# A hybrid diffusion block on one core: when the last squares are summed, where the first down piece lies, and how the last product ends

## The chip, the cores and the metric

The kernel runs on one core of one Trainium2 chip. The metric is the device time of one execution in microseconds (us), taken as the median of several runs. The engines are TensorE (PE in the profile; its weight loads are PEld), VectorE (DVE), ScalarE (ACT), GpSimd (POOL) and SyncE (SP), which here only issues DMAs. A matmul writes to PSUM, which has eight banks of 512 fp32 columns per partition; everything else lies in SBUF or in device memory.

## The reference

One layer of a diffusion backbone on 512 latent tokens and 256 context tokens, of width 1024:

```
h_lat = modulate(x, norm1_g, sh1, sc1)          # RMSNorm * (1 + scale) + shift
h_ctx = modulate(ctx, norm1_g, csh1, csc1)
o_lat = token_mixer(h_lat, h_ctx, ...)          # one input projection, then:
    ssd = rmsnorm(y_ssd * silu(z), ssd_norm_g)  #   bidirectional SSD, 4 groups, 2048 channels
    att = windowed attention + context + sink
    out = (sig_ssd * (ssd @ w_o_ssd) + sig_att * (att @ w_o_att)) @ w_out
x = x + gt1 * o_lat
x = x + gt2 * conv_ffn(modulate(x, norm2_g, sh2, sc2))   # up 1024 -> 2 x 2816, conv, silu gate, down
return rmsnorm(x, final_g)
```

The six modulation vectors come from `silu(c) @ w_mod + b_mod`.

## The kernel before

**Precision.** A product of two fp32 matrices is three matmuls: both operands are split in a high and a low part, and high x high, high x low and low x high are added (L193, L194 and L196 in `gemm`; L1861 to L1863 in `down`). A weight piece of 128 x 1024 is loaded on SP's queue into one of three raw buffers ("wraw"), then `split` makes the high part on ScalarE (L149) and the low part on VectorE (L150). High and low go to the buffers "whi" and "wlo", two of each, unless `ELSEWHERE` names another place for that piece. `run` walks a list of steps, each with the names of its weight pieces, and loads one piece ahead.

**Order.** Each engine works through its own instructions in order. PE's order is written out by hand in some stages (`tc.manual_schedule`), among them the whole of `down`. Elsewhere the order on an engine is chosen when the kernel is built, from program order and an estimate of when each instruction can start; `tc.keep_in_program_order` pins an instruction behind those pinned before it on its engine.

**SSD branch and its norm.** The gated rows yz of the SSD branch come in four groups of four row blocks. Their squares are summed into one tile, `ssq`: `square` lets ScalarE square a block (L1333) and GpSimd add it to `ssq` (L1336). For the last group (`late` false) these four squares stand next to the output projection.

**Output projection of the SSD branch.** `y_split` loads the sixteen blocks of yz, scales them and splits them to `yh` (ScalarE, L1525) and `yl` (VectorE, L1526). `os_first` computes the first two output row blocks in two passes over the channels; its PE order is written out. Piece ("os", 2) has its high and low part in a part of `yh[3]` that isn't filled yet, which is why its subtraction shows as `yh<-wraw,yh`. At the end of the first pass `rms_sums_of([ssq])` sums `ssq` over the partitions on PE (L238); root and spreading (L248, L249, L255) follow, giving `F["rs"]`. `os_step(o)` for o = 2 to 7 does the other row blocks: `merge_rows` loads three gate rows (ts_d, ta_d, ao_d) on SP, `gates` (L1540, L1541) combines them with `F["rs"]`, a gemm of 48 matmuls follows, then `merge`. Between these steps `weave` puts the steps on the modulation weights (`msteps[8:18]`): each loads a piece of w_mod (the raw buffer shows as `wraw<-wm`) and multiplies and adds it on VectorE (L554, L556).

**Feed-forward.** `up_step` runs 22 times, with the convolution on ScalarE and VectorE after its products (L1756 to L1758 read PSUM). `down` computes the down projection as seven products of half-size matrices (`ORDER` = p1, p3, p6, p7, p5, p2, p4), each of six weight pieces g = 0 to 5 and two token tiles t = 0, 1 (g = 5 has half the width): 42 `ITEMS`. `prepared(i)` loads and splits piece i up to `AHEAD` = 4 pieces ahead; the first piece, ("dn", 0), is split by `run` as any other, into "whi" and "wlo". `operand` gives the tokens' side, for some products loaded from device memory into a ring. `block` issues the matmuls of one piece on one tile, `product` those of one product. Each accumulator is one PSUM bank from `accb()`.

**The end.** The last product, p4, gives two tiles of 128 tokens x 512 columns. For each tile, behind all of PE's work: two VectorE operations (L1981, L1982), a square with its sum on ScalarE (L1904), `root` (L1916, L1917 on VectorE, L1918 on GpSimd), the scaling (L1985 on VectorE, L1987 on ScalarE for the columns that were finished before) and the output DMAs (L1922 in `put`).

Of the kernel before, what the change touches and what calls it, by code (L numbers as in the profile page):

```python
# [18 lines left out]
P = 128  # L19
# [25 lines left out]
def tile_hybrid_layer(  # L45
# [1276 lines left out]
    def square(late=True):  # L1322

        yz = SQUARES.pop(0)
        if "ssq" not in F:
            F["ssq"] = [ssq]
            tc.keep_in_program_order(S.activation(ssq, yz, AF.Square))
        else:

            tag = "th" if late or len(F["ssq"]) % 4 == 0 else "E"  # L1330
            sq = bp.tile([P, 512], F32, tag=tag, name="sq", bufs=3 if tag == "E" else 1)
            F["ssq"].append(sq)
            a = S.activation(sq, yz, AF.Square)  # L1333
            if late:
                tc.keep_in_program_order(a)
            G.tensor_tensor(ssq, ssq, sq, ALU.add)  # L1336
# [220 lines left out]
    def os_first(x):  # L1557

        def fn(*w):
            if x == 0:  # L1560
                F["os"] = accb(), accb()
            else:
                rows = [merge_rows(o) for o in range(2)]


            first = [(0, o, range(4)) for o in range(2)] if x else [(0, i % 2, (i // 2,)) for i in range(8)]
            with tc.manual_schedule(engines={mybir.EngineType.PE}):
                for u, o, ks in first + [(1, o, range(4, 8)) for o in range(2)]:
# [200 lines left out]

    ELSEWHERE["up", 1] = far_piece  # L1770

# [48 lines left out]
    def prepared(i):  # L1820
# [27 lines left out]
    def down(w0):  # L1848
# [5 lines left out]

        def block(i, bank, t, first, last):
            hi, lo, x = READY[i]
            n, g = ITEMS[i]
            for j in range(pairs(g)):
                h, l = x(j)
                z, r = slice(512 * j, 512 * j + 512), tok(t)  # L1860
                T.matmul(bank[t], h[:, r], hi[:, z], start=first and g == 0 and j == 0, stop=False, skip_group_check=True)  # L1861
                T.matmul(bank[t], l[:, r], hi[:, z], start=False, stop=False, skip_group_check=True)  # L1862
                T.matmul(bank[t], h[:, r], lo[:, z], start=False, stop=last and g == 5, skip_group_check=True)  # L1863

        def product(n, bank, first, last, between={}):
            i0 = 6 * ORDER.index(n)
            seq = [(g, t) for g in range(6) for t in range(2)]
            if n == "p4":
                seq = seq[:8] + [(g, t) for t in range(2) for g in range(4, 6)]
            for g, t in seq:  # L1870
                if t == 0:
                    for k in range(i0 + g, i0 + g + AHEAD):
                        if 1 < k < len(ITEMS) and k not in READY:
                            if ITEMS[k] == ("p2", 0):
                                space()
                            prepared(k)
                block(i0 + g, bank, t, first, last)
                if t == 1 and g in between:
                    between[g]()

# [8 lines left out]
        def space():  # L1889
            F["ring"] = F["c2"].tile([P, 2, NP2, HL], F32R, tag="xl", name="ring").rearrange("p a b c -> p (a b c)")  # L1890
            F["ring"] = F["ring"][:, : 4 * 1024].rearrange("p (r a b c) -> p r a b c", r=4, a=2, b=2)
            F["fg"] = F["c2"].tile([P, 2, NP2, HL], F32, tag="xh", name="fgb").rearrange("p a b c -> p (a b c)")[:, :D]
# [10 lines left out]
        def square_sum(t, c, y):  # L1903
            S.activation(tmp("tm"), y, AF.Square, accum_out=ss3[:, t, c : c + 1])  # L1904
            XO[t, c] = y
# [6 lines left out]

        def root(t):
            rs = cpool.tile([P, 4], F32, tag="rs", name="rs", bufs=2)[:, :1]
            ms = cpool.tile([P, 4], F32, tag="ms", name="ms", bufs=2)[:, :1]
            V.tensor_tensor(ms, ss3[:, t, 0:1], ss3[:, t, 1:2], ALU.add)  # L1916
            V.tensor_scalar(ms, ms, 1.0 / D, EPS, ALU.mult, ALU.add)  # L1917
            G.tensor_tensor(rs, ms, phalf[:, 0:1], ALU.pow)  # L1918
# [5 lines left out]
        def finish(t):  # L1924
            rs = root(t)
            for c in range(2):
# [3 lines left out]
        with tc.manual_schedule(engines={mybir.EngineType.PE}):  # L1930
            m = [accb(), accb()]
            product("p1", m, True, True)
            sa = snap(m, "tb")
            f_ = [accb(), accb()]
            product("p3", f_, True, True)
# [7 lines left out]
            for t in range(2):  # L1943
# [5 lines left out]
                {  # L1949
                    0: lambda: update(0, 1, f[0]),  # L1950
                    1: lambda: update(1, 1, f[1]),
                    2: lambda: update(2, 1, hs[0]),
                    3: lambda: update(3, 1, hs[1]),
                },
# [4 lines left out]
            def early(t):  # L1959
# [5 lines left out]
                V.tensor_tensor(y, y, F["fg"][:, CH[1]], ALU.mult)  # L1965

            def third():
# [7 lines left out]
            product(  # L1975
                "p4", h, False, True,
                {0: lambda: update(0, 0, sa[0]), 1: lambda: update(1, 0, sa[1]), 2: third, 3: fourth},
            )
            for t in range(2):
                y = XO[2 + t, 0] = tmp("ta")  # L1980
                V.tensor_tensor(y, h[t], F["g2"][0], ALU.mult)  # L1981
                V.tensor_tensor(y, y, sb[t], ALU.add)  # L1982
                square_sum(2 + t, 0, y)
                rs = root(2 + t)
                V.scalar_tensor_tensor(y, y, rs, F["fg"][:, CH[0]], ALU.mult, ALU.mult)  # L1985
                put(2 + t, 0)
                S.activation(XO[2 + t, 1], XO[2 + t, 1], AF.Copy, scale=rs)  # L1987
                put(2 + t, 1)

# [6 lines left out]
    def tok(t):  # L1996
# [101 lines left out]
```

## Time and profile before

| what | us |
|---|---|
| median of 3 runs | 1255.89 |
| the runs | 1256.02, 1255.89, 1253.77 |
| the profiled execution | 1256.97 |
| its span in the profile | 1255.2 |
| PE busy in the span | 1229.2 |
| VectorE busy | 920.6 |
| ScalarE busy | 683.2 |
| GpSimd busy | 174.7 |
| mean granted clock of TensorE | 0.995 |

Times in the profile count from the start of the span, so 749.09 means 749.09 us after it. A row of the timeline gives the start, the duration, the engine, the line of the kernel and the operation with its output and inputs, then how many of them follow each other (x3) and, in brackets, how long the engine sat idle before it and what ended that. A row of a group gives the number of instructions with their shortest, median and longest duration in ns. A row of windows gives the busy time of PE, PEld, DVE, ACT and POOL with the number of instructions, then the granted clock, the share of the DMA engines that was busy, and GB/s. A matmul's own duration is longer than the distance to the next, since matmuls are pipelined.

### The profile page before, as it was taken

Reading aid. Unit: us, or ns where it says so; the run is one execution under the profiler, and the core shown is the slowest. Engines: PE = TensorE matmul, PEld = TensorE weight load, DVE = VectorE, ACT = ScalarE, POOL = GpSimd, SP = SyncE. Lnnn points to the kernel's source line nnn. Section 1 sums busy time; section 2 is a strip of 40 time slices with the busy share of each in tenths; the row PEclk is TensorE's granted clock in tenths of the full one; section 3 lists DMA queues with packets and bytes.
Section 4 is the critical chain, followed back from the end, with each engine's and each line's share of the span. In section 5 each row is a group of like instructions: output and inputs, shape, how many; then the busy total and the mean of one; then the engine's idle time right before and its main releaser. Section 6 shows DMA issues by size and latency. Waiting matters only on the chain.

```text
span 1255.2 us, 17458 instructions
## 1 busy us (share of the span) xinstructions
PE 1229.2 (98%) x6292; PEld 1010.6 (81%) x6292; DVE 920.6 (73%) x1517; ACT 683.2 (54%) x1286; POOL 174.7 (14%) x177
## 2 busy tenths in 40 slices
PE   7999999999999999999999999999999999999997
PEld 4698888888888878778777777888988888887885
DVE  4856887888654697787787777777678888886566
ACT  3557887887445366475475654223545444445443
POOL 0000111121100034252452540000200000000000
PEclk9999999999999999999999999999999999999999
DMA  9652568877845234354355567777145444457685
GB/s 340 231 172 86 183 212 186 222 189 211 223 141 186 93 102 127 119 163 155 113 139 171 155 213 253 240 253 246 47 143 184 163 141 151 151 167 250 220 287 199
DMA packets 109494, 226.74 MB, mean 181 GB/s; under 512 B 9568, under 2 KB 48800, under 8 KB 109408
## 3 DMA queue, kind: packets, MB, share of 16 engines
q1 hardware_dynamic: 101920, 199.42, 48.8%
q0 software_dynamic: 6912, 25.17, 8.5%
q8 instruction: 49, 0.80, 0.3%
q10 hardware_dynamic: 576, 1.05, 0.2%
q14 instruction: 37, 0.30, 0.1%
HBM read 194.34 MB, written 50.92 MB: 195 GB/s over the span
## 4 chain that ended last, share of the span: by engine, by line
PE 84%; DVE 7%; POOL 3%; ACT 2%; DMA 2%; issue 2%; SPq 0%; POOLq 0%; DVEq 0%; ACTq 0%
PE acc L196 17%; PE acc L193 17%; PE acc L194 17%; PE acc L1861 3%; PE acc L1862 3%; PE acc L1863 3%; PE score L784 3%; PE po L833 3%; PE pt L820 2%; PE mis L408 2%; PE mis L1452 1%; PE mis L1446 1%; DVE wlo L150 1%; PE acc L903 1%; PE acc L904 1%
## 5 line engine op out<-in xcount | busy, mean ns | idle before, releaser
L150 DVE TENSOR_TENSOR wlo<-wraw,whi 128x1024 fp32r<-128x1024 f32 (+2 forms) x123 | 154.9, 1260 | 72.4 <-ACT whi L149 68.3
L193 PE MATMUL acc<-hlh,whi 128*128 128x512 f32 x488 | 200.1, 410 | 0.0
L196 PE MATMUL acc<-hlh,wlo 128*128 128x512 f32 x488 | 191.3, 392 | 0.0
L194 PE MATMUL acc<-hll,whi 128*128 128x512 f32 x488 | 190.8, 391 | 0.0
L149 ACT CAST whi<-wraw 128x1024 fp32r<-128x1024 f32 (+2 forms) x123 | 126.6, 1031 | 115.2 <-PE acc L194 62.1
L193 PE MATMUL acc<-mh,whi 128*128 128x512 f32 x368 | 143.7, 390 | 0.0
L196 PE MATMUL acc<-mh,wlo 128*128 128x512 f32 x368 | 143.2, 389 | 0.0
L194 PE MATMUL acc<-ml,whi 128*128 128x512 f32 x368 | 143.2, 389 | 0.0
L196 PEld LDWEIGHTS acc<-hlh,wlo 128*128 128x128 f32 x488 | 91.6, 188 | 20.2
L194 PEld LDWEIGHTS acc<-hll,whi 128*128 128x128 f32 x488 | 91.9, 188 | 18.2 <-issue 2.4
L193 PEld LDWEIGHTS acc<-hlh,whi 128*128 128x128 f32 x488 | 91.8, 188 | 17.7 <-issue 2.4
L194 PEld LDWEIGHTS acc<-ml,whi 128*128 128x128 f32 x368 | 69.1, 188 | 14.6 <-issue 0.2
L193 PEld LDWEIGHTS acc<-mh,whi 128*128 128x128 f32 x368 | 69.1, 188 | 14.5 <-issue 0.2
L196 PEld LDWEIGHTS acc<-mh,wlo 128*128 128x128 f32 x368 | 69.1, 188 | 14.3
L793 DVE CUSTOM_DVE_ANT_0 p<-score,winm,nsink 128x512 f32<-128x512 f32 (+1 forms) x64 | 51.9, 810 | 15.3 <-PE score L784 13.8
L1239 DVE SCALAR_TENSOR_TENSOR ta<-acc,half,ta 128x511 f32<-128x511 f32 (+1 forms) x66 | 43.8, 664 | 21.6 <-ACT ta L1238 21.5
L800 ACT ACTIVATE p<-p,mneg 128x512 f32<-128x512 f32 (+1 forms) x64 | 49.7, 777 | 15.4 <-DVE mneg L793 14.9
L1238 ACT ACTIVATE ta<-acc,half 128x512 f32<-128x512 f32 (+1 forms) x66 | 46.5, 705 | 20.8 <-PE acc L196 19.5
L193 PE MATMUL acc<-hch,whi 128*128 128x256 f32 x176 | 54.4, 309 | 0.0
L1357 POOL TENSOR_TENSOR st<-st,eT 128x512 f32<-128x512 f32 x24 | 29.2, 1218 | 177.3 <-ACT st L1374 159.2
L828 DVE TENSOR_TENSOR ptl<-pt,pth 128x512 fp32r<-128x512 f32 x72 | 47.5, 686 | 8.5 <-ACT pth L824 7.7
L556 DVE SCALAR_TENSOR_TENSOR tm<-wraw,csil,tm 128x512 f32<-128x512 f32 x56 | 41.9, 748 | 15.5 <-DMA wraw<-wm 14.9
(453 smaller groups left out, 2950.4 us busy)
## 6 DMA issues: line engine op xcount, KB each, us to landing
wraw<-wup SPq DMA_DIRECT2D x44, 512.0 KB, 3.9
wt_d<-wdn POOLq DMA_DIRECT2D x36, 512.0 KB, 7.8
fb<-cs_d SPq DMA_DIRECT2D x32, 512.0 KB, 5.9
wraw<-wm SPq DMA_DIRECT2D x32, 512.0 KB, 3.8
wraw<-wx SPq DMA_DIRECT2D x24, 512.0 KB, 3.5
wraw<-wt_d SPq DMA_DIRECT2D x20, 512.0 KB, 4.4
sp_d<-te SPq DMA_DIRECT2D x33, 256.0 KB, 2.1
wm<-wm SPq DMA_DIRECT2D x16, 512.0 KB, 8.0
```

Source lines behind the costliest of these rows:

```text
L149: S.copy(hi[:, :n], r[:, :n])
L150: V.tensor_tensor(lo[:, :n], r[:, :n], raw(hi[:, :n]), ALU.subtract)
L193: T.matmul(ps, wh, xh[:, k0 + k, :], start=a, stop=False)
L194: T.matmul(ps, wh, xl[:, k0 + k, :], start=False, stop=False)
L196: T.matmul(ps, wl, xh[:, k0 + k, :], start=False, stop=b)
L556: V.scalar_tensor_tensor(acc, r[:, u * 512 : u * 512 + 512], sc, acc, ALU.mult, ALU.add)
L784: T.matmul(ps[:, o : o + len(z) * P], Q[h][:, b * P : (b + 1) * P], k[:, j, z[0] * P : (z[-1] + 1) * P], start=v == 0 and o % 512 in (0, P ...
L793: V.tensor_tensor_reduce(p[:, :w], d["ps"][i][:, o0 : o0 + w], m, op0=ALU.add, op1=ALU.min, scale=1.0, scalar=nsink[:, h : h + 1], accum_o ...
L800: S.activation(p, p, AF.Exp, bias=d["mneg"][:, i : i + 1], scale=-1.0, accum_out=d["den"][:, i : i + 1])
L828: V.tensor_tensor(d["ptl"][x], d["pt"][x], raw(d["pth"][x]), ALU.subtract)
L1238: S.activation(o[:, :n], ps[:, :n], AF.Identity, scale=hcol(base_w, stride + i), bias=hcol(base_b, i))
L1239: V.scalar_tensor_tensor(o[:, 1:n], ps[:, 0 : n - 1], hcol(base_w, i), o[:, 1:n], ALU.mult, ALU.add)
```

## The change

The diff touches four places.

1. `square` for the last group: the four squares go to temporary tiles and GpSimd adds none of them. In `os_first(0)`, VectorE adds them to `ssq` just ahead of `rms_sums_of`, pinned to program order.
2. The list of steps: `os_step(2)` and `os_step(3)` stand without modulation steps, and `msteps[8:18]` are woven among `os_step(4)` to `os_step(7)`.
3. `("dn", 0)` gets its high and low part from `far_piece` (two "ww" buffers of another pool), as does the last piece; the accumulators of p1 and p3 are taken in another order, so that each gets another bank; the ring of operands has six places, and p4 prepares six pieces ahead.
4. p4 runs g = 0, 1 on both tiles, then g = 2 to 5 on tile 0, then g = 2, 3 on tile 1, then g = 4, 5 on tile 1 for columns 0 to 255 and again for columns 256 to 511. The finishing of tile 0 is called behind its last block, that of each column half of tile 1 behind its own. The square takes a scale of 1/32, so that its sum is already the mean over 1024, and `root` is one VectorE operation and one on GpSimd.

```diff
         else:
-            tag = "th" if late or len(F["ssq"]) % 4 == 0 else "E"
-            sq = bp.tile([P, 512], F32, tag=tag, name="sq", bufs=3 if tag == "E" else 1)
-            F["ssq"].append(sq)
-            a = S.activation(sq, yz, AF.Square)
-            if late:
-                tc.keep_in_program_order(a)
+            if not late:
+                sq = tmp(("te", "tc")[len(F["ssq"]) % 2])
+                S.activation(sq, yz, AF.Square)
+                F["ssq"].append(sq)
+                return
+            sq = bp.tile([P, 512], F32, tag="th", name="sq", bufs=1)
+            tc.keep_in_program_order(S.activation(sq, yz, AF.Square))
             G.tensor_tensor(ssq, ssq, sq, ALU.add)
...
             if x == 0:
+                for sq in F["ssq"][1:]:
+                    tc.keep_in_program_order(V.tensor_tensor(ssq, ssq, sq, ALU.add))
                 F["rm"] = rms_sums_of([ssq], 4, 1, 4.0 * EPS, late=True)
...
-    ELSEWHERE["up", 1] = far_piece
+    ELSEWHERE["up", 1] = ELSEWHERE["dn", 0] = far_piece
...
-        if i % 5 < 2:
+        if i == len(ITEMS) - 1:
+            hi, lo = far_piece()
+        elif i % 5 < 2:
...
-                x = F["ring"][:, i % 4]
+                x = F["ring"][(g if n == "p2" else g + 2) % 4 if ITEMS[i] < ("p4", 4) else g]
...
-        def block(i, bank, t, first, last):
+        def block(i, bank, t, first, last, cols=slice(0, 512)):
...
-                z, r = slice(512 * j, 512 * j + 512), tok(t)
...
+                z, r = slice(512 * j + cols.start, 512 * j + cols.stop), tok(t)
+                b, end = bank[t][:, cols], last and g == 5
...
             if n == "p4":
-                seq = seq[:8] + [(g, t) for t in range(2) for g in range(4, 6)]
+                seq = seq[:4] + [(g, t) for t in range(2) for g in range(2, 6)]
             for g, t in seq:
                 if t == 0:
-                    for k in range(i0 + g, i0 + g + AHEAD):
+                    for k in range(i0 + g, i0 + g + (6 if n == "p4" else AHEAD)):
...
+                if n == "p4" and t == 1 and g == 4:
+                    break
                 block(i0 + g, bank, t, first, last)
-                if t == 1 and g in between:
-                    between[g]()
+                if (g, t) in between:
+                    between[g, t]()
+            if n == "p4":
+                for u, z in enumerate(HALF):
+                    for g in (4, 5):
+                        block(i0 + g, bank, 1, first, last, z)
+                    between[5, 1, u]()
...
-            S.activation(tmp("tm"), y, AF.Square, accum_out=ss3[:, t, c : c + 1])
+            S.activation(tmp("tm"), y, AF.Square, scale=1.0 / 32.0, accum_out=ss3[:, t, c : c + 1])
...
-        def root(t):
+        def root(a, b, eps=EPS):
...
-            V.tensor_tensor(ms, ss3[:, t, 0:1], ss3[:, t, 1:2], ALU.add)
-            V.tensor_scalar(ms, ms, 1.0 / D, EPS, ALU.mult, ALU.add)
+            V.tensor_scalar(ms, a, b, eps, ALU.add, ALU.add)
             G.tensor_tensor(rs, ms, phalf[:, 0:1], ALU.pow)
...
-            m = [accb(), accb()]
+            m, f_ = [accb()], [accb()]
+            m.append(accb())
             product("p1", m, True, True)
             sa = snap(m, "tb")
-            f_ = [accb(), accb()]
+            f_.append(accb())
             product("p3", f_, True, True)
...
+            def result(t, z, acc):
+
+                y = XO[2 + t, 0]
+                V.tensor_tensor(y[:, z], h[t][:, z], F["g2"][0][:, z], ALU.mult)
+                V.tensor_tensor(y[:, z], y[:, z], sb[t][:, z], ALU.add)
+                S.activation(tmp("tm")[:, z], y[:, z], AF.Square, scale=1.0 / 32.0, accum_out=acc)
+
+            def scaled(t, rs):
+                y = XO[2 + t, 0]
                 V.scalar_tensor_tensor(y, y, rs, F["fg"][:, CH[0]], ALU.mult, ALU.mult)
                 put(2 + t, 0)
                 S.activation(XO[2 + t, 1], XO[2 + t, 1], AF.Copy, scale=rs)
                 put(2 + t, 1)
...
+            def fifth():
+                XO[2, 0] = tmp("ta")
+                result(0, slice(0, 512), ss3[:, 2, 0:1])
+                scaled(0, root(ss3[:, 2, 0:1], ss3[:, 2, 1:2]))
+
+            def sixth():
+                XO[3, 0] = tmp("ta")
+                result(1, HALF[0], ss3[:, 3, 0:1])
+                V.tensor_scalar(ss3[:, 0, 0:1], ss3[:, 3, 0:1], ss3[:, 3, 1:2], EPS, ALU.add, ALU.add)
+
+            def last():
+                result(1, HALF[1], ss3[:, 0, 1:2])
+                scaled(1, root(ss3[:, 0, 1:2], ss3[:, 0, 0:1], 0.0))
+
+            product(
+                "p4", h, False, True,
+                {
+                    (0, 1): lambda: update(0, 0, sa[0]), (1, 1): lambda: update(1, 0, sa[1]),
+                    (2, 0): third, (4, 0): fourth, (5, 0): fifth, (5, 1, 0): sixth, (5, 1, 1): last,
+                },
+            )
...
-        + weave([os_step(o) for o in range(2, 8)], msteps[8:18])
+        + [os_step(o) for o in range(2, 4)]
+        + weave([os_step(o) for o in range(4, 8)], msteps[8:18])
```

More of the change, by code (lines that the diff above doesn't have):

```diff
@@ L1859, in block, with product @@
                 h, l = x(j)
-                z, r = slice(512 * j, 512 * j + 512), tok(t)
[L1861 to L1865, printed above, removed]
+                z, r = slice(512 * j + cols.start, 512 * j + cols.stop), tok(t)
+                b, end = bank[t][:, cols], last and g == 5
+                T.matmul(b, h[:, r], hi[:, z], start=first and g == 0 and j == 0, stop=False, skip_group_check=True)
+                T.matmul(b, l[:, r], hi[:, z], start=False, stop=False, skip_group_check=True)
+                T.matmul(b, h[:, r], lo[:, z], start=False, stop=end, skip_group_check=True)
+        def product(n, bank, first, last, between={}, halves=None):
             i0 = 6 * ORDER.index(n)
@@ L1890, in space @@
             F["ring"] = F["c2"].tile([P, 2, NP2, HL], F32R, tag="xl", name="ring").rearrange("p a b c -> p (a b c)")
-            F["ring"] = F["ring"][:, : 4 * 1024].rearrange("p (r a b c) -> p r a b c", r=4, a=2, b=2)
+            F["ring"] = [
+                F["ring"][:, 1024 * r : 1024 * r + 512 * n].rearrange("p (a b c) -> p a b c", a=n, b=2)
+                for r, n in enumerate((2, 2, 2, 2, 2, 1))
+            ]
             F["fg"] = F["c2"].tile([P, 2, NP2, HL], F32, tag="xh", name="fgb").rearrange("p a b c -> p (a b c)")[:, :D]
@@ L1924, in finish @@
         def finish(t):
-            rs = root(t)
+            rs = root(ss3[:, t, 0:1], ss3[:, t, 1:2])
             for c in range(2):
@@ L1949, in down @@
                 {
[L1950 to L1953, printed above, removed]
+                    (0, 1): lambda: update(0, 1, f[0]),
+                    (1, 1): lambda: update(1, 1, f[1]),
+                    (2, 1): lambda: update(2, 1, hs[0]),
+                    (3, 1): lambda: update(3, 1, hs[1]),
                 },
@@ L1965, in early @@
                 V.tensor_tensor(y, y, F["fg"][:, CH[1]], ALU.mult)
+            def result(t, z, acc):
[5 more added lines that the diff above has]
+                y = XO[2 + t, 0]
+                V.scalar_tensor_tensor(y, y, rs, F["fg"][:, CH[0]], ALU.mult, ALU.mult)
+                put(2 + t, 0)
+                S.activation(XO[2 + t, 1], XO[2 + t, 1], AF.Copy, scale=rs)
+                put(2 + t, 1)
             def third():
```

11 lines of the change are left out of this document (removed).

## The prediction

> **What bounds the kernel now.** The page comes first: span, and busy time of each engine.
>
> ```profile
> span 1255.2 us, 17458 instructions
> ...
> PE 1229.2 (98%) x6292; PEld 1010.6 (81%) x6292; DVE 920.6 (73%) x1517; ACT 683.2 (54%) x1286; POOL 174.7 (14%) x177
> ```
>
> TensorE is busy for all but 1255.2 - 1229.2 = 26.0 us. The change removes no matmul, so all that it can win lies in idle PE, in a lowered clock while PE is busy, and behind the last matmul. The second view is the list of PE's waits (what PE waited for, total us, times, longest):
>
> ```profile
> PE acc L196 <- DVE yh L150: 2.3, 1, 2.3
> PE acc L196 <- DVE wlo L150: 1.6, 1, 1.6
> ```
>
> Both are in the output projection of the SSD branch, where the change moves work; the other edited places have waits under 1 us, shown with their parts below. The third view is a table of windows around the first (window, length, busy us of each engine, granted clock, DMA share, GB/s):
>
> ```profile
> 750.00:752.00 2.00, 0.21 (x1) 0.22 (x2) 2.00 (x3) 1.68 (x3) 0.04 (x1) 1.00 1.05 402
> 752.00:754.00 2.00, 2.00 (x6) 1.58 (x6) 2.00 (x4) 2.00 (x5) 0.00 (x0) 0.57 0.90 307
> 754.00:756.00 2.00, 2.00 (x7) 1.55 (x7) 2.00 (x3) 2.00 (x4) 0.00 (x0) 0.58 0.96 314
> ```
>
> The first window holds the idle PE; in the next two PE is busy at a clock of 0.57 and 0.58. Those 4 us do (1 - 0.575) x 4 = 1.7 us less work than at full clock, so the stall costs more than its own length.
>
> **Squares of the last gated rows.** Four squares (ScalarE, then GpSimd's add into the sum) are followed now by four VectorE adds, pinned later. The rows: GpSimd's adds, VectorE's low halves (L1526) with and without these adds beside them, and the timeline (start us, us, engine, line).
>
> ```profile
> L1336 POOL TENSOR_TENSOR ssq<-ssq,sq x15: 1267/1297/2363, 555.4 to 748.4; 128x512 f32<-128x512 f32 x15
> ...
> L1526 DVE SCALAR_TENSOR_TENSOR yl<-ld,vec,yh x12: 740/744/752, 751.7 to 764.3; 128x512 fp32r<-128x512 f32 x12
> L1526 DVE SCALAR_TENSOR_TENSOR yl<-ta,vec,yh x3: 1721/1764/1782, 745.5 to 748.8; 128x512 fp32r<-128x512 f32 x3
> ...
> 748.87 0.39 PE L193 MATMUL acc<-yh,yh 128*128 128x512 f32 x1
> 749.09 0.39 PE L194 MATMUL acc<-yl,yh 128*128 128x512 f32 x1
> 750.52 1.21 DVE L150 TENSOR_TENSOR yh<-wraw,yh 128x1024 fp32r<-128x1024 f32 x1
> 751.78 0.50 PE L196 MATMUL acc<-yh,yh 128*128 128x512 f32 x1 [2.31 <-DVE yh L150]
> 755.01 1.22 DVE L150 TENSOR_TENSOR wlo<-wraw,whi 128x1024 fp32r<-128x1024 f32 x1
> 758.55 1.47 DVE L1526 SCALAR_TENSOR_TENSOR yl<-ld,vec,yh 128x512 fp32r<-128x512 f32 x2 [0.33 <-ACT yh L1525]
> 763.27 0.94 PE L238 MATMUL mis<-rmsc,ssq 128*128 128x1 f32 x8
> ```
>
> Three L1526 take 1764 ns while GpSimd adds, twelve take 744 ns once it is done: 3 x 1.02 = 3.1 us. Behind them on VectorE stands the subtraction of 750.52 (the low half of the weight piece that lies in yh[3]), and PE waits for it. Matmuls start 0.22 to 0.23 us apart (748.87, 749.09), so 749.09 to 751.78 costs 2.69 - 0.23 = 2.46 us; with the clock, 4.2 us. Without GpSimd the subtraction runs 747.5 to 748.7, ahead of PE's need at 749.3: the whole stall goes, and the lowered clock with it.
>
> What is late next is the sum itself. L238 reads it at 763.27; PE 4.2 us earlier reaches that at 759.1. Four 128x512 adds take 4 x 0.69 = 2.8 us (each as the row of 1247.25 in the tail, below). They are pinned behind the second weight piece's subtraction, which ends at 756.2. At once, they end at 759.0: no wait. But the y_split of the last block is ahead of them in program order, and its low halves run from 756.16 to 760.0, the last two held by ScalarE and a load (0.33 at 758.55); these 744-ns pieces are ready at about the same times as now. If the adds come among them, the sum is ready near 762.1 and PE waits 3.0 us there. Bounds for the part: 4.2 - 0 = 4.2, and 4.2 - 3.0 - 1.7 (clock drops again) = -0.5. I take 4.2 - 3.0 = 1.2, because VectorE is full from 750 to 756 and has more waiting. The squares' buffers are now held until the adds, so two prefetches of x into them go later; x is next read after all eight output steps, which hide them, and I cost that at nothing (two 256-KB loads on SP, if the cover failed).
>
> The trace has one idle stretch of 2.31 us followed by 3.4 us at half clock, and one of 1.57 us (777.76, below) with none, so an idle 3.0 us may cost 1.7 us more. [...]
>
> **Modulation steps moved.** The list of steps is re-woven: output steps 2 and 3 now stand without the steps on the modulation weights (wm), and all ten lie among steps 4 to 7.
>
> ```profile
> 774.53 0.49 DVE L554 TENSOR_SCALAR tm<-wraw,csil 128x512 f32<-128x512 f32 x1 [2.32 <-DMA wraw<-wm]
> 775.88 0.69 DVE L1541 SCALAR_TENSOR_TENSOR ld<-ld,r_s 128x512 f32<-128x512 f32 x1 [0.26 <-DMA ld<-ts_d]
> 776.49 1.22 DVE L150 TENSOR_TENSOR wlo<-wraw,whi 128x1024 fp32r<-128x1024 f32 x1
> 777.76 0.50 PE L196 MATMUL acc<-yh,wlo 128*128 128x512 f32 x1 [1.57 <-DVE wlo L150]
> ...
> 787.00:798.00 11.00, 11.00 (x50) 9.13 (x49) 8.80 (x12) 2.73 (x3) 0.00 (x0) 1.00 0.74 244
> ...
> L556 DVE SCALAR_TENSOR_TENSOR tm<-wraw,csil,tm 128x512 f32<-128x512 f32 x56 | 41.9, 748 | 15.5 <-DMA wraw<-wm 14.9
> ...
> wraw<-wm SPq DMA_DIRECT2D x32, 512.0 KB, 3.8
> ```
>
> VectorE stands in order: it waits 2.32 us for a wm load, then for the gate rows ts_d, and only then makes the low half that PE lacks (1.57 us idle, some 1.7 with the restart). With no wm load there, VectorE isn't held, and the gate rows land sooner by 512 KB at 244 GB/s = 2.1 us; the subtraction then ends near 775.6 instead of 777.7. PE can therefore leave this place at most about 2.1 us earlier than now, whatever it won before: 1.2 and 1.7 don't add. Between 1.2 and 2.1 I take **1.8** for both together, nearer to the bound of the place that comes last. Bounds: -0.5 (above) and 4.0, where the gate rows too come earlier by what PE and VectorE won.
>
> What it adds: steps 4 to 7 get 2.5 wm loads each instead of 1.67. One output step is 48 matmuls x 0.227 = 10.9 us. It brings two weight pieces, three gate rows of 256 KB and the wm pieces: (2 + 2.5) x 0.524 + 0.786 = 3.14 MB, or 289 GB/s, against 249 now; VectorE gets 0.83 x 2 x 0.75 us (L556) = 1.25 us more on 8.80 of 11 us. Both fit under PE: DMA went to 402 GB/s in the window 750:752, and 8.8 + 1.25 is less than 11. I cost it at nothing; without that cover it is the slower rival below.
>
> **First down piece in idle buffers, another bank.**
>
> ```profile
> 1134.52 1.04 ACT L149 CAST whi<-wraw 128x1024 fp32r<-128x1024 f32 x1 [0.95 <-PE acc L194]
> 1135.95 0.40 PE L1862 MATMUL acc<-whi,fyl 128*128 128x512 f32 x1
> 1136.87 0.50 PE L1863 MATMUL acc<-wlo,fyh 128*128 128x512 f32 x1 [0.53 <-DVE wlo L150]
> 1137.67 0.39 PE L1863 MATMUL acc<-wlo,fyh 128*128 128x512 f32 x1
> 1138.65 1.21 DVE L150 TENSOR_TENSOR dnw<-wraw,dnw 128x1024 fp32r<-128x1024 f32 x1
> 1138.88 0.47 PE L1861 MATMUL acc<-whi,fyh 128*128 128x512 f32 x1 [0.82 <-DVE tc L1758]
> ```
>
> ScalarE's cast waits until PE lets go of the up weights in whi; the subtraction follows and PE waits for it. In the "ww" buffers nothing is waited for. The second wait is for a PSUM bank that the last up step's VectorE line still reads (L1758); the change gives that bank to the third accumulator, first used a whole product later. Start to start, 1135.95 to 1136.87 loses 0.92 - 0.23 = 0.69 us, and 1137.67 to 1138.88 loses 1.21 - 0.23 = 0.98; the slower restarts (0.1 each) bring it to **1.85**. Next late would be the third piece, the first in the dnw buffers: its subtraction ends at 1139.9 (row 1138.65). Two pieces of 12 matmuls come ahead of it, 24 x 0.227 = 5.4 us from about 1135.6, so PE wants it at 1141.0 at the earliest: covered by 1.1 us, and if it were not, that much would come back. Bounds 0.7 (the bank alone keeps its wait) and 1.9.
>
> **The tail.** The last product ends tile by tile, and for the last tile in two halves of 256 columns (nine matmuls a half, 18 in place of 9), with one small VectorE operation fewer in the root.
>
> ```profile
> 1246.10 0.39 PE L1863 MATMUL acc<-wlo,ring 128*128 128x512 f32 x1
> 1246.52 0.69 DVE L1981 TENSOR_TENSOR ta<-acc,g 128x512 f32<-128x512 f32 x1 [0.63 <-PE acc L1863]
> 1247.25 0.69 DVE L1982 TENSOR_TENSOR ta<-ta,te 128x512 f32<-128x512 f32 x1
> 1248.04 0.63 ACT L1904 ACTIVATE tm<-ta 128x512 f32<-128x512 f32 x1 [1.32 <-DVE ms L1917]
> 1249.39 0.15 DVE L1916 TENSOR_TENSOR ms<-bp 128x1 f32<-128x1 f32 x1
> 1249.88 0.54 POOL L1918 TENSOR_TENSOR rs<-ms,phalf 128x1 f32<-128x1 f32 x1 [1.19 <-DVE ms L1917]
> 1250.45 0.75 DVE L1985 SCALAR_TENSOR_TENSOR ta<-ta,rs,fgb 128x512 f32<-128x512 f32 x1 [0.72 <-POOL rs L1918]
> ...
> 1141.52 0.42 DVE L1737 TENSOR_TENSOR tb<-tb,ta 128x256 f32<-128x256 f32 x1
> ...
> 894.39 2.25 PE acc L1781 x18
> ```
>
> From PE's end (1246.5) to the end of the last L1985 (1251.2) are 4.7 us now. After: two half-width VectorE steps of 0.42 (row 1141.52) instead of 0.69, a half square (0.3) with its read of the sum (0.19), one small step (0.15), GpSimd 0.54, L1985 0.75, and the gaps between engines: about 3.2. So 1.5 less, if PE's second half follows the first at once. PE itself pays 2.25 us for 18 such matmuls (row 894.39, there too of 256 columns) against 9 x 0.227 = 2.04: +0.2. The unknown is whether PE may write columns 256 to 511 while VectorE reads 0 to 255 of the same bank; no row shows it. If it must wait, it loses the 0.42 read, 0.04 to start, and what VectorE has first (the other tile's L1985, 0.75): 0.6 to 1.2. That leaves 1.5 - 0.2 - (0 to 1.2) = 0.1 to 1.3; add 0.3 because two output transfers instead of four remain at the end: 0.4 to 1.6. I take **0.75**, nearer to waiting.
>
> [...]
>
> **Sum.** 1.8 + 1.85 + 0.75 = 4.4 us off 1256.97 (the profiled execution, span 1255.2 plus 1.8 around it): 1252.6. The median shown is 1255.89, 1.1 below that execution, so **1251.5**.
>
> **Rivals.**
> 1. The adds come in time and the gate rows follow: the first two parts give 4.0, so 1249.3, or 1248.5 with a full tail. For it: the adds could end at 759.0, just PE's time. Against: VectorE is idle there for 0.33 us only (758.55).
> 2. PE waits at L238 long enough to drop the clock: -0.5 there, with the later stall as a bound near 0: 1253.3 to 1253.8. For it: 2.31 us idle did so at 751.78.
> 3. The change doesn't do what it says in the tail: the second half waits for the first's read, 0 to 0.4 instead of 0.75: 1251.9 to 1252.3.
> 4. **Slower**: packed wm loads bind steps 4 to 7. At 244 GB/s (the window quoted) 3.14 MB take 12.9 us, 2.0 more than PE's 10.9: 4 x 2.0 = 8 us lost, 1251.5 + 8 = 1259.5. It decides from (4.4 + 2.5) / 4 = 1.7 us a step, that is below 250 GB/s. For it: VectorE is held by late wm loads as at 774.53. Against: 0.74 DMA share at 244 makes 330 at full share.
>
> **How the numbers follow.** Forecast 0.46 (1250.3 to 1253), rival 1 0.15, rival 2 0.16, rival 3 0.08, rival 4 0.08, and 0.07 for nothing gained in the first two parts and little elsewhere (1254 to 1257). A measurement of this kernel can tell 0.2%, 2.5 us. Below 1253.4 lie nearly all of the forecast and rivals 1 and 3 and a third of rival 2: faster 0.72; slower 0.09; the same 0.19. The range reaches from rival 1 to past rival 2, 1248.0 to 1255.0, leaving out rival 4, most of the last case and a little below.
>
> **What would show it.** L1526 all near 744 ns and no wait at the weights in yh[3]: the first step right. A PE wait at L238 for VectorE of 2 to 3 us: the adds are late, as forecast; a clock under 0.6 there: rival 2. No PE wait of 1.6 us at the fifth output step's weights: the move works; several new waits for L150 between 780 and 825: rival 4. No waits at L1861 to L1863 at the start of down: 1.85 holds. In the tail, PE idle between the two halves tells rival 3. Wrong altogether if new PE waits show outside these places.

## The result, and the profile after

The changed kernel takes 1263.48 us, the kernel before 1256.26 us, each the median of six runs (1259.97 to 1265.03, and 1253.77 to 1257.19): a ratio of 1.0056, 95% interval 1.0041 to 1.0072. It is slower by 7.2 us where 4.4 us less were forecast, and lies outside the range. The profiled execution took 1263.1 us with a span of 1261.3 us, 6.1 more than that of before.

The page of the changed kernel, busy us of each engine:

```profile
span 1261.3 us, 17466 instructions
...
PE 1232.1 (98%) x6301; PEld 1012.8 (80%) x6301; DVE 920.7 (73%) x1520; ACT 683.5 (54%) x1288; POOL 167.7 (13%) x173
```

Two things are to be seen. PE is idle for 29.2 us now and was for 26.0; it is also busy for 2.9 us more, though only nine short matmuls came in; a part of that is matmuls at half clock: before its last matmul the clock is lowered for 10.2 us now and was for 6.8, which is 1.7 us of work. And VectorE's total is what it was (920.6 us): four adds went to it, and the slowing down by GpSimd's adds went away. Its list of waits of PE (what for, total us, times, longest):

```profile
PE acc L193 <- ACT whi L149: 3.2, 3, 2.4
PE mis L238 <- DVE ssq L1576: 3.2, 1, 3.2
PE acc L196 <- DVE wlo L150: 2.0, 4, 0.5
PE acc L1867 <- DVE ta L1986: 0.9, 1, 0.9
...
PE acc L1867 <- DVE tc L1761: 0.7, 1, 0.7
```

The two waits of before in the output projection (2.3 us for `yh L150`, 1.6 us for `wlo L150`) are gone; the second line is the wait for the sum, the first and third are seven new waits from 821 to 856, the last two are the tail and the start of down.

**The sum of squares.** The low halves, the adds and PE's wait in the timeline and the groups of the changed kernel, then its windows:

```profile
L1527 DVE SCALAR_TENSOR_TENSOR yl<-ta,vec,yh x3: 747/747/752, 744.0 to 745.3; 128x512 fp32r<-128x512 f32 x3
...
757.28 0.69 DVE L1576 TENSOR_TENSOR ssq<-ssq,tc 128x512 f32<-128x512 f32 x1
...
762.36 0.69 DVE L1576 TENSOR_TENSOR ssq<-ssq,te 128x512 f32<-128x512 f32 x1
...
763.20 1.84 PE L238 MATMUL mis<-rmsc,ssq 128*128 128x1 f32 x8 [3.19 <-DVE ssq L1576]
```

```profile
762.00:764.00 2.00, 0.80 (x4) 0.83 (x5) 1.71 (x3) 0.00 (x0) 0.00 (x0) 0.76 1.06 387
764.00:766.00 2.00, 2.00 (x8) 1.81 (x9) 0.83 (x2) 0.00 (x0) 0.69 (x1) 0.50 0.86 330
766.00:768.00 2.00, 2.00 (x6) 1.55 (x5) 0.69 (x1) 0.00 (x0) 0.80 (x1) 0.50 0.52 155
768.00:770.00 2.00, 2.00 (x6) 1.57 (x5) 0.00 (x0) 0.00 (x0) 0.00 (x0) 0.54 0.99 372
```

The three low halves take 747 ns instead of 1764, so the stall at 749 went. But the four adds are spread from 757.28 to 763.05 among other work, PE waits 3.19 us, and the granted clock (the third number from the right, 0.76 to 0.50) is lowered for longer than before: 2 x (0.24 + 0.50 + 0.50 + 0.46) = 3.4 us lost.

**The packed modulation steps.** Three of the seven new waits (1.3 us) stand at the start of output steps 6 and 7, four (3.9 us) in the first two steps of the out projection behind them, whose weight pieces (`wraw<-wout`) pass through the same three raw buffers. The longest of them in the changed kernel's timeline, SP's and VectorE's rows from the modulation loads on, then ScalarE's and PE's, and the window around it:

```profile
831.57 2.49 SPq L145 DMA_DIRECT2D wraw<-wm  x2
...
838.02 0.33 SPq L145 DMA_DIRECT2D wraw<-wm  x1
...
845.38 1.22 DVE L150 TENSOR_TENSOR wlo<-wraw,whi 128x1024 fp32r<-128x1024 f32 x1 [5.33 <-ACT whi L149]
...
846.63 0.33 SPq L145 DMA_DIRECT2D wraw<-wm  x1
...
848.91 0.75 DVE L556 SCALAR_TENSOR_TENSOR tm<-wraw,csil,tm 128x512 f32<-128x512 f32 x1
...
849.68 0.33 SPq L145 DMA_DIRECT2D wraw<-wout  x1
...
853.22 1.04 ACT L149 CAST whi<-wraw 128x1024 fp32r<-128x1024 f32 x1 [4.16 <-DMA wraw<-wout]
...
854.31 0.50 PE L193 MATMUL acc<-mh,whi 128*128 128x512 f32 x1 [2.38 <-ACT whi L149]
```

```profile
842.00:853.00 11.00, 8.93 (x39) 6.55 (x38) 7.52 (x12) 1.67 (x2) 0.00 (x0) 1.00 0.38 134
```

The second load of the row at 831.57 and the one at 838.02 bring the last two of the ten moved pieces. They hold two of the three raw buffers while VectorE, in order, stands idle for 5.33 us before the subtraction of a weight piece. That subtraction frees the third buffer at 846.60, and one more modulation piece takes it (846.63). VectorE finishes with the first of the two pieces at 849.66; 20 ns later SP issues the load of the next weight piece; 3.5 us after that it is cast, and PE has waited 2.38 us for it. The DMA engines are busy for 0.38 of this window and VectorE for 7.52 of 11 us.

**The start of down and the tail**, from the same timeline:

```profile
1145.21 0.47 PE L1867 MATMUL acc<-ww,fyh 128*128 128x512 f32 x1 [0.75 <-DVE tc L1761]
...
1252.28 0.42 DVE L1986 TENSOR_TENSOR ta<-acc,g 128x256 f32<-128x256 f32 x1
...
1252.75 0.39 PE L1867 MATMUL acc<-whi,ring 128*128 128x256 f32 x1 [0.95 <-DVE ta L1986]
...
1256.58 0.75 DVE L1992 SCALAR_TENSOR_TENSOR ta<-ta,rs,fgb 128x512 f32<-128x512 f32 x1 [0.72 <-POOL rs L1933]
```

The wait for the weights at the start of down is gone, the wait for the bank is not. And PE's second column half waits for VectorE's read of the first.

### The profile page after: what moved, and what is told of

Read it like the earlier page. It is cut to its first block, busy times and chain, and to the rows that moved or that the text cites. A ratio compares the mean times of both kernels' runs of the same rounds, so it can differ in the third digit from the quotient of the medians.

```text
span 1261.3 us, 17466 instructions
## 1 busy us (share of the span) xinstructions
PE 1232.1 (98%) x6301; PEld 1012.8 (80%) x6301; DVE 920.7 (73%) x1520; ACT 683.5 (54%) x1288; POOL 167.7 (13%) x173
## 4 chain that ended last, share of the span: by engine, by line
PE 79%; DVE 9%; ACT 3%; DMA 3%; POOL 2%; issue 2%; SPq 0%; POOLq 0%; ACTq 0%; DVEq 0%
PE acc L196 16%; PE acc L194 16%; PE acc L193 16%; PE score L784 3%; PE po L833 3%; PE pt L820 2%; PE acc L1867 2%; PE acc L1868 2%; PE acc L1869 2%; PE mis L408 2%; DVE wlo L150 1%; PE mis L1453 1%; PE mis L1447 1%; PE acc L903 1%; PE acc L905 1%
## 5 line engine op out<-in xcount | busy, mean ns | idle before, releaser
L150 DVE TENSOR_TENSOR wlo<-wraw,whi 128x1024 fp32r<-128x1024 f32 (+2 forms) x121 | 152.8, 1263 | 78.0 <-ACT whi L149 68.8
L556 DVE SCALAR_TENSOR_TENSOR tm<-wraw,csil,tm 128x512 f32<-128x512 f32 x56 | 42.7, 763 | 13.6 <-DMA wraw<-wm 12.9
```

The costliest lines, as they stand in the source:

```text
L150: V.tensor_tensor(lo[:, :n], r[:, :n], raw(hi[:, :n]), ALU.subtract)
L556: V.scalar_tensor_tensor(acc, r[:, u * 512 : u * 512 + 512], sc, acc, ALU.mult, ALU.add)
```

## The experiments

Each kernel ran beside the kernel before on the same chip; the ratios are against that.

### The list of steps: e1 and e2

e1 is the changed kernel with the old list:

```diff
-        + [os_step(o) for o in range(2, 4)]
-        + weave([os_step(o) for o in range(4, 8)], msteps[8:18])
+        + weave([os_step(o) for o in range(2, 8)], msteps[8:18])
```

> The changed kernel (1263.5) with its list of steps as before: the modulation steps woven among output steps 2 to 7 again. Theory 1 (the packed modulation steps cost about 8.5 us between 798 and 860, and what they bought is the 1.7-us stall at the fifth piece): 1263.5 - 8.5 + (0 to 1.7), so 1255 to 1256.7. Rival (the wait at the sum of squares with its two lowered clock windows is the main loss): 1260 or more.

e2 is the kernel before with the opposite edit.

> The kernel before (1256.3) with the new list of steps and nothing else. Theory 1 (the packing alone costs about 8.5 us and saves about 1.7): 1262 to 1264. Rival (the packing hurts only together with the held temporaries of the squares, whose prefetches of x go later): within 2 us of before, 1254 to 1258.

e1: 1255.3 us, ratio 0.9996 (0.9986 to 1.0005). e2: 1263.1 us, ratio 1.0059 (1.0040 to 1.0078). One window of e1 and the same of e2:

```profile
842.00:853.00 11.00, 11.00 (x50) 9.12 (x49) 9.06 (x11) 3.72 (x5) 0.00 (x0) 1.00 0.76 246
```

```profile
842.00:853.00 11.00, 8.33 (x30) 5.94 (x28) 7.78 (x13) 2.71 (x3) 0.00 (x0) 0.84 0.42 130
```

The list alone makes the kernel slower by as much as the whole change does, and taking it back gives 8.2 us. Theory 1 holds for the loss, both rivals fall. What the list bought is less plain. In e1, with the old list, there is no wait at 776 either; PE comes there late, after its wait at L238. In e2 the subtraction at that place ends at 775.53, where the prediction had 775.6, but PE now gets there earlier and still waits for it. Rows of e2's timeline:

```profile
774.31 1.22 DVE L150 TENSOR_TENSOR wlo<-wraw,whi 128x1024 fp32r<-128x1024 f32 x1
...
775.58 0.50 PE L196 MATMUL acc<-yh,wlo 128*128 128x512 f32 x1 [1.20 <-DVE wlo L150]
```

e1 also says that the other edits together are worth nothing measurable; its trace still has 3.1 us of wait at L238 and a lowered clock behind it (0.50 from 766 to 768).

### Bytes, buffers, density: e4, e11, e12, e10

e4 gives the modulation pieces of this stage two places outside the three raw buffers:

```diff
-        r = wpool.tile([P, 1024], F32, tag="raw", name="wraw", bufs=3)
+        if key[0] == "m" and 8 <= key[1] < 18:
+            r = x1[1].rearrange("p a c -> p (a c)")[:, key[1] % 2 * 1024 : key[1] % 2 * 1024 + 1024]
+        else:
+            r = wpool.tile([P, 1024], F32, tag="raw", name="wraw", bufs=3)
```

> The changed kernel, with the ten packed modulation loads in two buffers of their own (memory that is written only in the out projection) instead of the three raw buffers of the weight pieces; DMA bytes and VectorE work are the same. Theory 2 (the loss between 798 and 860 comes from the three raw buffers, which the modulation pieces hold until VectorE reaches them, so that weight pieces are loaded late): the loss goes, 1254 to 1257. Rival (DMA bandwidth or VectorE's load bind): stays, 1261 to 1264.

1259.63 us, ratio 1.0030 (1.0018 to 1.0042): half of the loss went, and neither number was met. The stage has no wait left, here a window and a row of e4's DMA queue:

```profile
842.00:853.00 11.00, 11.00 (x52) 9.07 (x52) 7.23 (x12) 2.98 (x4) 0.00 (x0) 1.00 0.57 177
```

```profile
739.56 3.65 SPq L148 DMA_DIRECT2D x<-wm  x2
```

But the row shows that this is no clean test: with free buffers the first modulation loads go out at 739.56, in front of the loads of yz, and PE's wait for the sum grows to 4.2 us. Fewer loads are left among the packed steps, so buffers and density aren't told apart here.

e11 and e12 start from e9 (below), which has no wait in this stage with 2.0 modulation loads a step. e11 adds bytes that use neither raw buffers nor VectorE:

```diff
+            if 2 <= o < 7:
+                x = x1[1].rearrange("p a c -> p (a c)")[:, o % 2 * 1024 : o % 2 * 1024 + 1024]
+                S.copy(x[:, 0:1], raw(mh[:, o, 0:1]))
+                S.dma_start(x, src["m", 8][0])
```

> As e9 (1247.7), and in output steps 2 to 6 one more load of 512 KB each, of weights that nobody reads, from ScalarE's queue into memory that nobody else uses then: 3.4 MB a step with the 2.0 modulation loads, more than the 3.14 MB of the changed kernel; the three raw buffers and VectorE's order are as in e9. Theory 2 (not the bytes bind the packed steps, but pieces that wait for one of three raw buffers and for VectorE): waits between 780 and 860 under 1 us in sum, within 1 us of e9. Rival (bytes: loads land later when more is moved): waits of 3 us or more there, 1250.5 or more.

e12 is e9 with the changed kernel's list.

> As e9, with the changed kernel's list of steps (none among output steps 2 and 3, ten among steps 4 to 7, 2.5 a step, 3.14 MB). Theory 2: the waits between 798 and 860 come back though nothing else is late here, 5 to 8.5 us more than e9, 1253 to 1256. Rival (the packed steps cost only because PE came late and out of step after the wait at the sum of squares): within 1.5 us of e9.

e11: 1250.61 us, ratio 0.9970 (0.9952 to 0.9988), 2.9 more than e9. e12: 1256.4 us, ratio 1.0004 (0.9991 to 1.0016), 8.7 more than e9. Windows of e11, then of e12:

```profile
798.00:809.00 11.00, 10.95 (x51) 8.84 (x50) 9.98 (x17) 2.91 (x4) 0.00 (x0) 1.00 0.98 353
...
820.00:831.00 11.00, 11.00 (x52) 9.10 (x51) 8.95 (x15) 3.04 (x5) 0.00 (x0) 1.00 0.98 341
831.00:842.00 11.00, 9.27 (x40) 7.06 (x39) 4.82 (x7) 2.09 (x2) 0.00 (x0) 1.00 0.64 204
```

```profile
820.00:831.00 11.00, 8.69 (x35) 6.30 (x35) 9.21 (x14) 2.07 (x3) 0.00 (x0) 0.96 0.83 264
831.00:842.00 11.00, 11.00 (x45) 8.96 (x44) 4.74 (x6) 2.20 (x3) 0.00 (x0) 0.88 0.59 199
842.00:853.00 11.00, 8.63 (x36) 6.47 (x35) 9.74 (x15) 2.20 (x3) 0.00 (x0) 0.90 0.61 183
```

In e11 neither expectation holds as a whole: the time is the rival's (1250.5 or more), the 2.3 us of PE waits lie between the two. So bytes do cost something. The waits (at 815.99, 839.30 and 840.56) come behind the two windows in which the DMA engines are full (0.98), and by another pattern, here in e11's timeline:

```profile
829.87 0.33 SPq L145 DMA_DIRECT2D wraw<-wout  x1
...
838.20 1.04 ACT L149 CAST whi<-wraw 128x1024 fp32r<-128x1024 f32 x1 [8.68 <-DMA wraw<-wout]
```

This weight piece goes out in time (e9's goes out at 829.52 and is cast at 833.90) and is cast 8.3 us later, because its load lands late; the one of the changed kernel went out late and was cast 3.5 us later. From 787 to 853 e11 moves 281 GB/s, e12 222 and the changed kernel 213, and e11 loses less than e12: 2.9 us by the medians (4.8 by the ratios), against 8.7 (9.0). In e12 the waits come with the DMA engines at 0.6 to 0.8, after the pattern of the changed kernel; its trace, of the slowest of ten executions, has 4.7 us of waits there, and 5.1 us lost by a lowered clock. In its timeline:

```profile
844.75 0.75 DVE L556 SCALAR_TENSOR_TENSOR tm<-wraw,csil,tm 128x512 f32<-128x512 f32 x1
845.53 0.33 SPq L145 DMA_DIRECT2D wraw<-wout  x1
...
849.02 1.04 ACT L149 CAST whi<-wraw 128x1024 fp32r<-128x1024 f32 x1 [4.12 <-DMA wraw<-wout]
...
850.12 0.50 PE L193 MATMUL acc<-mh,whi 128*128 128x512 f32 x1 [1.86 <-ACT whi L149]
```

L556 ends at 845.50, the load goes out at 845.53. So the packed list loses by pieces that hold raw buffers until VectorE comes to them; PE's lateness at L238 isn't needed for it: e12 has no wait there. How much of the 8.7 us is the number of buffers and how much VectorE's order was not separated.

e10 is e6 (below) with 2.0 loads a step.

```diff
-        + weave([os_step(o) for o in range(2, 8)], msteps[8:18])
+        + [os_step(2)]
+        + weave([os_step(o) for o in range(3, 8)], msteps[8:18])
```

> As e6 (1251.6) with the modulation steps woven over output steps 3 to 7, 2.0 a step. Theory (three raw buffers carry 2 + 2.0 pieces a step, as a piece holds a buffer for about 7 us and a step has 10.9): no waits between 780 and 860, the 0.7 us at 774 goes, 1250.5 to 1251. Rival (the packing binds in proportion, half of the 8.5 us that 2.5 a step cost): 1254 to 1256.

1252.62 us, ratio 0.9970 (0.9959 to 0.9981), against 1251.62 of e6: waits of 0.7, 0.4 and 0.5 us appear between 788 and 820. The theory's range was missed by 1.6 us, and the rival's by 1.4; the same list costs nothing in e9, where VectorE's order is another. 2.0 a step is at the edge.

### The place of the adds: e3 and e8, e7

e3 is e1 with L238 and the spread one block later in PE's order:

```diff
                     if u == 2 and o:
+                        F["rm"] = rms_sums_of([ssq], 4, 1, 4.0 * EPS)
+                    if u == 3 and not o:
                         F["rs"] = in_sbuf(rms_spread(F["rm"], 4), 4, "r_s")
...
-                F["rm"] = rms_sums_of([ssq], 4, 1, 4.0 * EPS, late=True)
```

> As e1, and PE sums the squares (L238) one block of 12 matmuls later and spreads the root one block later, so that VectorE's adds end before PE asks for them. Theory 1 (3.35 us of wait and 3.4 us of lowered clock at that place belong to the late adds alone): 1248 to 1250, no wait at L238 and full clock at 760 to 770. Rival (VectorE is the bound there, and the wait moves to the spread or to the next weight piece): 1253 to 1256.

1253.61 us, ratio 0.9980 (0.9970 to 0.9989). The wait at L238 is gone (it starts at 766.45 without one) and no lowered clock shows up to there (the matmuls start 0.23 us apart up to 766.22), as theory 1 has it, but the time is the rival's, and so is a new wait at the next weight piece. Rows of e3's timeline:

```profile
762.14 0.69 DVE L1578 TENSOR_TENSOR ssq<-ssq,tc 128x512 f32<-128x512 f32 x1
762.74 1.22 DVE L150 TENSOR_TENSOR wlo<-wraw,whi 128x1024 fp32r<-128x1024 f32 x1
...
764.01 0.50 PE L196 MATMUL acc<-yh,wlo 128*128 128x512 f32 x1 [1.65 <-DVE wlo L150]
```

The next weight piece's subtraction stands behind three of the adds, and PE waits for that.

e8 adds the squares after the last low halves, puts L238 behind the second pass and the spread one block into output step 2, and with it the merges of the first two row blocks (from e5, below):

```diff
-                for sq in F["ssq"][1:]:
-                    tc.keep_in_program_order(V.tensor_tensor(ssq, ssq, sq, ALU.add))
...
+    def add_squares():
+        for sq in F["ssq"][1:]:
+            tc.keep_in_program_order(V.tensor_tensor(ssq, ssq, sq, ALU.add))
...
-        + [os_first(0), ([], lambda: y_split(range(12, 16))), os_first(1)]
+        + [os_first(0), ([], lambda: y_split(range(12, 16))), ([], add_squares), os_first(1)]
```

> As e5, and VectorE adds the squares only after the last low halves of yz, with L238 behind the whole second pass and the spread one block into output step 2. Theory (the 1.65-us wait at 762 in e3 is the third weight piece's subtraction standing behind the adds; VectorE has the same work, it only stands in the way elsewhere): no wait near 762, 1.0 to 1.8 us less than e5 if no new wait appears. Rival (VectorE is short of time in this whole stretch, as it has the adds' 2.8 us in place of the 3.1 us that GpSimd cost it): a wait of similar size appears after 765, the sum within 0.7 us of e5.

1255.0 us, ratio 0.9992 (0.9980 to 1.0003): 3.2 more than e5, a miss for both. There is no wait at 762, as the theory has it, and a larger one later, in e8's timeline:

```profile
773.20 0.49 DVE L554 TENSOR_SCALAR tm<-wraw,csil 128x512 f32<-128x512 f32 x1 [2.74 <-DMA wraw<-wm]
...
775.66 0.79 PE L196 MATMUL acc<-yh,wlo 128*128 128x512 f32 x1 [4.63 <-DVE wlo L150]
```

VectorE stands 2.74 us before a modulation load with the weight pieces' subtractions behind it: the wait that the change's list was to remove.

e7 is e5 with e4's buffers and the old list.

> As e5, with the modulation loads of these output steps in two buffers of their own, woven over output steps 2 to 7 as before. Theory (with three raw buffers shared, a late modulation load holds VectorE and with it the weight piece: the waits of 0.4 and 0.9 us near 774 and 791 in e3): those two go, 1.6 us less than e5. Rival (they come from the gate rows or from VectorE's order): unchanged within 0.5 us, or moved.

1255.36 us, ratio 1.0001 (0.9989 to 1.0014), 3.6 more than e5, a miss: as in e4 two modulation loads go out before the loads of yz, VectorE gets its blocks later, and PE waits 3.4 us for a weight piece at 767.61 (in a trace of the slowest of ten executions).

### Down: e5 and e6

e5 is e3 with another order of the first product:

```diff
+            if n == "p1":
+                seq = [(g, t) for t in range(2) for g in range(2)] + seq[4:]
```

> As e3 (1253.6), and p1 takes its first two pieces on tile 0 before either on tile 1, so that the second accumulator's bank is first written 12 matmuls later. Theory (the 0.75-us wait at the start of down is still for the bank that the last up step's VectorE line reads; asking for the accumulators in another order did not give tile 1 another bank): the wait goes, 0.9 to 1.0 us less in the trace, 1252.6. Rival (the wait comes from the split of the next pieces on VectorE, and only its name is the bank's): a wait of about 0.7 us stays at the second or third piece, 1253.6.

1251.79 us, ratio 0.9964 (0.9951 to 0.9977). No wait is left at the start of down. The waits of e3 near 774 (0.4 us) and 791 (0.9) also went, but for 0.2 us, without an edit there, so not all of the 1.8 us is the bank's.

e6 is e5 with the last tile in one piece: `result` on columns 0 to 511, no `sixth`, no halves.

> As e5, and the last tile ends in one piece of 512 columns instead of two halves. Theory (PE's second half waits 0.95 us for VectorE's read of the first, so the halves win almost nothing): within 0.5 us of e5, from the end of PE to the end of the span about 1.4 us more and the end of PE about 1.2 us earlier. Rival (the halves bring most of the 0.75 us forecast or more): e6 slower than e5 by 0.8 to 1.5 us.

1251.62 us, ratio 0.9962 (0.9948 to 0.9976), 0.2 us from e5: the halves bring nothing that can be measured.

### All together: e9

e9 is e8 with e6's whole tile and e10's list.

> As e8 with the whole last tile of e6, and output step 2 alone without modulation steps (ten over steps 3 to 7, 2.0 a step, between 1.67 of the kernel before and 2.5 of the changed one). Theory (the 4.6-us wait of e8 is VectorE waiting 2.7 us for a modulation load with the weight piece's subtraction behind it): that wait goes with no new one above 0.5 us, full clock at 770 to 780, 1249 to 1250. Rival (2.0 loads a step bind the three raw buffers already, or the late adds still hold the weight piece): new waits between 780 and 860 of 2 us or more in sum, 1252 or more.

1247.67 us, ratio 0.9932 (0.9915 to 0.9950), below both kernels and 1.3 under what the theory expected. The windows of e9 where the others wait:

```profile
776.00:787.00 11.00, 11.00 (x50) 9.09 (x50) 10.97 (x18) 3.98 (x5) 0.00 (x0) 1.00 0.70 244
787.00:798.00 11.00, 11.00 (x50) 9.13 (x49) 8.38 (x12) 2.72 (x3) 0.00 (x0) 1.00 0.81 279
...
842.00:853.00 11.00, 11.00 (x52) 9.10 (x51) 6.66 (x10) 3.21 (x4) 0.00 (x0) 1.00 0.60 197
```

From 654 us to its last matmul PE has no wait of 0.4 us or more and runs at full clock (1.00 in every window from 776 to 864; the mean over the whole span is 0.999). VectorE does the same work as in e12.

## Why the prediction was wrong

| step | forecast, us | measured in the trace, us |
|---|---|---|
| stall and clock at 749 to 756 | -4.2 | -4.2 |
| wait at L238 | +3.0 | +3.3 |
| clock behind it | 0 (bound +1.7) | +3.4 |
| stall at 776 | -1.7, the two places -1.8 in all | -1.7 |
| packed modulation steps | 0 | +8 |
| start of down | -1.85 | -1.2 |
| tail | -0.75 | -0.2 |
| start-up and a wait at 388, not touched | 0 | -1.5 |

These add up to +5.9, against 6.1 between the spans. They compare one execution of each kernel. The +8 is 5.2 us of PE waits (3.2 + 2.0 in the list), about 1 us of slower restarts (an estimate: from 854.31 to the next start are 0.34 us, where 0.23 is usual), and 1.7 us of lowered clock at 855.

**The step that failed** is "I cost it at nothing" for the moved modulation steps. It reckoned with throughput: 289 GB/s under the 402 of the window 750:752, 10.1 us of VectorE under 11. In the changed kernel neither binds: from 787 to 853 the DMA engines are busy for 0.65 of the time at 213 GB/s, VectorE for 43.3 of 66 us. What binds is that a weight piece needs one of three raw buffers, that modulation pieces keep theirs until VectorE reaches them, and that VectorE stands in order before another weight piece meanwhile (5.33 us at 845.38). How the loss divides between the number of buffers and VectorE's order stays open. A row that pointed at this was quoted in the prediction, 15.5 us of VectorE's idle time in front of L556 over the whole kernel, most of it for wm loads; nothing was drawn from it for these steps. Rival 4 named the sign and, with 8 us, the price, and got 0.08. Its mechanism was another: 2.0 us in each of steps 4 to 7, for want of bandwidth, where the trace has no wait in steps 4 and 5 and most of it behind step 7. That the sums agree is a coincidence.

**The adds.** The wait of 3.0 us at L238 was forecast and came (3.19). The bound of the clock was too small: one lowered stretch was reckoned, and two came, back to back. That the clock stays at full behind a wait of 3.0 us, as the 1.2 of the forecast has it, no run shows; the trace has 3.19 us idle followed by 6.8 us at half clock, and 2.38 us at 854 by another 3.4. And VectorE was reckoned as won: GpSimd's adds cost it 3.1 us, its own adds 2.75. In e3 the adds then stand before a weight piece's subtraction (1.65 us of wait); in e9, behind the last low halves, they cost no wait.

**The first down piece.** The cast and the split came off PE's path as forecast. That the second tile would get another bank was read from the code and not from a row; PE still waits 0.75 us for L1761. Asking for it 12 matmuls later does it (e5).

**The tail.** Rival 3 is what happened: PE waits 0.95 us for L1986, which reads other columns of the same bank. Whether it must, or only does in the kernel as built, no run shows, nor what the halves would win without that wait. The 0.75 was the author's choice between 0.4 and 1.6; measured are 0.2. The rest behind PE came as forecast, 3.2 us from its end (1254.1) to the end of the last L1992 (1257.33). The 0.3 us for fewer output transfers came from no row and didn't show: from there to the end of the span are 4.0 us, as in the kernel before (1251.20 to 1255.2).

**Right** were the 744 ns of L1526 without GpSimd, the end of the stall at 749, and the wait that would be late next. The end of the stall at 776 was right in size, but by luck: e1 has it with the old list, where PE comes there late, and e2, with the new list alone, still has 1.20 us of it.

## What to carry to other kernels

Busy shares don't tell what a queue of few buffers costs (here the DMA engines at 0.65, VectorE at 43.3 of 66 us, and 5.2 us of PE waits): count the pieces that pass through them per step, how long each is held, and which in-order engine lets it go; a piece that is not urgent holds a place that an urgent one needs. Moving work between engines that slow each other down may leave the sum as it was (a low half on VectorE took 1764 ns beside GpSimd's adds and 747 without them, and VectorE's total was 920.6 us and is 920.7), so look for the place where it stands in nobody's way, in front of nothing that PE is about to ask for. A wait that is removed is worth its length only if the next engine in line isn't late by itself, and here a removed wait brought its gain only after the third place behind it had been cleared too (e3, e8, e9).

## What was not expected of the hardware

In these traces the length of a PE wait alone doesn't tell how long the clock is lowered behind it. The same wait, for the weights in yh[3], was 2.31 us long in the kernel before and lowered the clock for 3.4 us (the windows in the prediction); in e2 it was 2.30 us long and left the clock at full. e2's window behind it:

```profile
752.00:754.00 2.00, 2.00 (x11) 1.63 (x10) 2.00 (x4) 2.00 (x5) 0.00 (x0) 1.00 0.76 282
```

Behind 1.65 us (e3, at 764.01) the matmuls start 0.23 to 0.24 us apart again after the first, as at full clock. 1.8 us (e12), 2.38 us (after) and 3.1 us (e1) lowered the clock for 3.4 us, 3.19 us (after) and 1.86 us (e12) for 6.8 us; behind 3.40 us (e7, at 767.61) the matmuls start 0.43 us apart, where 0.23 is usual. Behind the waits of 1.8, 1.86 and 2.38 us a second one of 0.5 us came within 1.3 us, which may count too. In the traces of before and after, each lowered stretch ahead of the last matmul has a granted clock of 0.50 and lasts 3.4 us (before: 38.89 to 42.30 and 752.27 to 755.69; after: 855.19 to 858.60) or 6.8 us (after: 763.03 to 769.86). As an estimate from these, a wait of 2 us costs 2 us, 3.7 us or 5.4 us, and its length doesn't tell which. So 1.7 of the 4.2 us won at 749 to 756 hang on the execution that was profiled.
